# Chunk products of a state-space layer laid on two halves of TensorE's columns

## The chip, the cores and the metric

The kernel runs on one core of one Trainium2 chip. The metric is device time in microseconds of one execution. A profiled execution gives, beside its own time, a trace of every engine: TensorE (PE for its matmuls, PEld for its weight loads), VectorE (DVE), ScalarE (ACT), GpSimd (POOL) and the queue that issues DMAs (SP). The span is the time from the first to the last instruction of that execution.

## The reference, cut to what matters

A sequence of 512 tokens with 1024 features goes through one Mamba-2 layer, a shared key/value projection, one layer of differential attention and a final norm, all in float32. The change lies in the Mamba-2 layer's scan. It has 8 groups of 4 heads, 64 values a head and a state of 128. Within a chunk, with `cb` the product of C and B and `decay` the causal decay between two tokens, the reference computes

```python
cb = jnp.einsum("blgn,bsgn->blsg", c_c, b_c)
y_diag = jnp.einsum("blsgr,bsgrp->blgrp", cb[..., None] * decay, x_c)
y_off = jnp.einsum("blgn,bgrpn->blgrp", c_c, state) * jnp.exp(acs)[..., None]
```

The reference scans chunks of 64 tokens. The kernel does the same sum over chunks of 128 tokens, 4 of them in the sequence. The change is in the product that gives `y_diag`, of a 128 x 128 matrix (source tokens by output tokens) with 128 x 64 values.

## The kernel before, in words

Everything runs on one core. Large projections (`pz`, `pg`, `po`, `pq`, `pk`, `pt`, `pv`, `pb`, `pc`) are computed as three products each of operands split into a high and a low part in the format fp32r (`mm3`, line 217). ScalarE writes the high part of a weight tile (`whi`), VectorE the low one (`wlo`). The smaller products of the scan are plain f32; the profile shows each of these as two weight loads and two matmuls, and each fp32r product as one of either.

The work of the scan is in `ssd(g)` (line 536), called once for each of the 8 groups (lines 629 to 631). In between, a generator (`stream_a`, line 505) supplies the projections in the order of `order_a` (line 90). The projections of the group that comes next and the output projections are independent of the running scan, so TensorE has them to work on while other engines prepare the scan's operands. Most of the order on each engine in this first part is set by the planner of the tile framework, which simulates the program when it is built and puts each engine's instructions into a fixed queue; a few stretches are kept in program order by hand (`Ordered`, lines 43 to 58).

In `ssd(g)`:

- `pcb` (lines 542 to 545) holds B and C multiplied, 128 x 128 for each of the 4 chunks.
- `decays` (line 516) has filled `dec` with the causal decays of 4 heads and 4 chunks; VectorE multiplies `pcb` into it (lines 565 and 566).
- `xdt` (line 559) holds the scaled values, with 128 source tokens on the partitions and 64 values a head.
- `bt`, `xe`, `psA`, `psB` and `hst` (lines 546 to 579) carry the state from chunk to chunk.
- Lines 584 to 591 form the products inside a chunk. A bank `pyd` of PSUM holds two chunks: for each of its 2 chunks and 4 heads, one product takes `dec[:, h, c, :]` as the stationary operand (128 source tokens by 128 output tokens) and moves `xdt[:, c, h, :]` (128 source tokens by 64 values). The result has 128 output tokens on the partitions and 64 columns. After 8 products VectorE adds the bank to `dx` (line 591).
- `po1` and `po2` (lines 595 to 599) give the part that comes from the state; the rest of the function gates, normalizes and transposes the result (`pyt`, line 622) into `yT` for the output projection.

Eight groups with two banks each make 16 banks `pyd` and 128 products. Nearly all instructions carry line 53 in the profile, the line of the recording helper, so the tiles' names tell them apart.

Of the kernel before, what the change touches and what calls it, by code (L numbers as in the profile page):

```python
# [24 lines left out]
HD = 64  # L25
# [36 lines left out]
def trunk(ctx, tc, x, x_t, par, w_dt, w_in, w_out, w_kvqg, w_bo, d_skip, lam_qk, fin_g, out):  # L62
    nc = tc.nc
    V, A, T = (Ordered(tc, e) for e in (nc.vector, nc.scalar, nc.tensor))
# [14 lines left out]
    def ss_bank(name):  # L79
        turns[0] += 1  # L80
        tag = "mm" if turns[0] % turns[1] >= 3 else "ss"
        return psum.tile([P, 512], F32, tag=tag, name=name, bufs=3 if tag == "ss" else 4)
# [453 lines left out]
    def ssd(g):  # L536
        bc, cc, x0, x1 = conv_out.pop(g)
        xc = (x0, x1)
        dec, een = decs.pop(g)
# [11 lines left out]
        xdt = bp.tile([P, NQ, R, HD], F32, tag="xdt", name=f"xdt{g}")  # L551
# [31 lines left out]
        pyd = []  # L583
        for q in range(2):
            pyd.append(ss_bank(f"pyd{g}_{q}"))
            for c in (2 * q, 2 * q + 1):
                for h in range(R):
                    o = (c % 2) * 256 + h * HD
                    T.matmul(pyd[q][:, o:o + HD], lhsT=dec[:, h, c, :], rhs=xdt[:, c, h, :], start=True, stop=True)
            dq = dx[:, 2 * q:2 * q + 2].rearrange("p c h e -> p c (h e)")  # L590
            V.tensor_tensor(out=dq, in0=pyd[q].rearrange("p (c e) -> p c e", c=2), in1=dq, op=ALU.add)
        if g % 2 and g < G - 1:
# [36 lines left out]
    for g in range(G):  # L629
        until(f"g{g}")  # L630
        ssd(g)
# [266 lines left out]
    def half(t, n):  # L898
        hs = slice(n * 512, (n + 1) * 512)
        return x_tok[:, t, hs], fg[:, hs], ot[t][:, hs], out[t * P:(t + 1) * P, hs]  # L900
# [45 lines left out]
    h = DH - 1  # L946
# [53 lines left out]
    y, f, o, dst = half(3, 0)  # L1000
# [69 lines left out]
```

## Time and profile before

| | before |
|---|---|
| median of 3 runs | 741.71 us (741.63 to 741.74) |
| the profiled execution's own time | 741.54 us |
| its span, first to last instruction | 739.4 us |
| TensorE matmuls busy, instructions | 725.5 us, 3741 |
| weight loads busy, instructions | 606.6 us, 3741 |
| VectorE busy | 531.6 us |
| ScalarE busy | 444.8 us |
| GpSimd busy | 114.7 us |
| mean granted TensorE clock | 0.998 |

Busy time counts the time in which at least one instruction of the engine is under way. Matmuls are pipelined: a matmul's duration reaches from its start to a modelled end, and the next one starts before that end. So a row's mean duration is longer than the distance between two starts, and the distance is what a row of matmuls costs. In the form of a TensorE row, "128\*128" is the part of the array that it uses (rows by columns) and "128x64" what it moves (partitions by columns). In a timeline row the first number is the start and the second the time until the end of the last of the instructions merged into it.

### The profile page before, as it was taken

Reading aid. Unit: us, or ns where it says so; the run is one execution under the profiler, and the core shown is the slowest. Engines: PE = TensorE matmul, PEld = TensorE weight load, DVE = VectorE, ACT = ScalarE, POOL = GpSimd, SP = SyncE. Lnnn points to the kernel's source line nnn. Section 1 sums busy time; section 2 is a strip of 40 time slices with the busy share of each in tenths; the row PEclk is TensorE's granted clock in tenths of the full one; section 3 lists DMA queues with packets and bytes.
Section 4 is the critical chain, followed back from the end, with each engine's and each line's share of the span. In section 5 each row is a group of like instructions: output and inputs, shape, how many; then the busy total and the mean of one; then the engine's idle time right before and its main releaser. Section 6 shows DMA issues by size and latency. Waiting matters only on the chain.

```text
span 739.4 us, 10330 instructions
## 1 busy us (share of the span) xinstructions
PE 725.5 (98%) x3741; PEld 606.6 (82%) x3741; DVE 531.6 (72%) x1197; ACT 444.8 (60%) x969; POOL 114.7 (16%) x158
## 2 busy tenths in 40 slices
PE   9999999999999999999999999999999999999995
PEld 7787878888887888887888879888898898888874
DVE  5479955799668669469896655666767857785876
ACT  6749763765819457256443357666766766755565
POOL 0108241402234141150110101000000000000002
PEclk9999999999999999999999999999999999999999
DMA  8533313134131323132213220331221131121002
GB/s 310 215 129 160 114 58 115 57 114 171 58 114 58 115 114 100 72 115 80 92 58 113 74 97 8 114 114 58 66 106 57 58 115 58 58 104 68 28 1 113
DMA packets 12914, 70.83 MB, mean 96 GB/s; under 512 B 1600, under 2 KB 2112, under 8 KB 5312
## 3 DMA queue, kind: packets, MB, share of 16 engines
q1 hardware_dynamic: 12576, 70.06, 26.2%
q8 instruction: 29, 0.48, 0.3%
q14 instruction: 21, 0.17, 0.1%
q10 hardware_dynamic: 288, 0.12, 0.1%
HBM read 68.02 MB, written 2.16 MB: 95 GB/s over the span
## 4 chain that ended last, share of the span: by engine, by line
PE 77%; DVE 8%; ACT 7%; issue 5%; DMA 2%; POOL 1%; SPq 0%; ACTq 0%; POOLq 0%
PE pg L53 15%; PE po L53 13%; PE pt L53 7%; PE pz L53 7%; PE pq L53 6%; PE pv L53 6%; PE pk L53 6%; PE pyd L53 4%; PE pb L53 3%; PE sc L53 3%; DVE wlo L53 2%; PE pc L53 2%; ACT whi L53 2%; ACT L53 2%; DVE xc L53 1%
## 5 line engine op out<-in xcount | busy, mean ns | idle before, releaser
L53 DVE SCALAR_TENSOR_TENSOR wlo<-raw,prm,whi 128x512 fp32r<-128x512 f32 (+1 forms) x256 | 150.2, 634 | 51.2 <-ACT whi L53 50.8
L53 ACT ACTIVATE whi<-raw,prm 128x512 fp32r<-128x512 f32 (+1 forms) x256 | 136.8, 605 | 58.4 <-PE pz L53 14.1
L53 PE MATMUL pg<-a_hi,whi 128*128 128x512 f32 x256 | 102.5, 402 | 0.5 <-DVE xc L53 0.4
L53 PE MATMUL pg<-a_hi,wlo 128*128 128x512 f32 x256 | 102.7, 405 | 0.0
L53 PE MATMUL pg<-a_lo,whi 128*128 128x512 f32 x256 | 101.4, 397 | 0.0
L53 DVE SCALAR_TENSOR_TENSOR xc<-pg,prm,xc 128x511 f32<-128x511 f32 (+2 forms) x96 | 69.9, 741 | 5.6 <-ACT xc L53 4.8
L53 PEld LDWEIGHTS pg<-a_hi,whi 128*128 128x128 f32 x256 | 48.2, 188 | 11.9 <-issue 0.8
L53 PEld LDWEIGHTS pg<-a_hi,wlo 128*128 128x128 f32 x256 | 48.1, 188 | 10.9
L53 PEld LDWEIGHTS pg<-a_lo,whi 128*128 128x128 f32 x256 | 48.2, 188 | 10.7
L53 PE MATMUL po<-whi,yh 128*128 128x512 f32 x128 | 51.0, 401 | 0.6 <-ACT yh L53 0.6
L53 PE MATMUL po<-wlo,yh 128*128 128x512 f32 x128 | 51.0, 401 | 0.4 <-DVE wlo L53 0.4
L53 PE MATMUL pz<-wlo,a_hi 128*128 128x512 f32 x128 | 50.9, 398 | 0.0
L53 PE MATMUL pz<-whi,a_lo 128*128 128x512 f32 x128 | 50.9, 399 | 0.0
L53 PE MATMUL pz<-whi,a_hi 128*128 128x512 f32 x128 | 49.8, 402 | 0.1
L53 PE MATMUL po<-whi,yl 128*128 128x512 f32 x128 | 50.0, 397 | 0.0
L53 ACT ACT_TABLE_LOAD x33 | 42.3, 1283 | 10.3 <-DVE xc L53 7.7
L916 POOL TENSOR_TENSOR ot<-ot,fg 128x512 f32<-128x512 f32 x4 | 5.5, 1400 | 257.9 <-ACT ot L53 257.9
L53 ACT ACTIVATE s<-s,mx 128x128 f32<-128x128 f32 (+3 forms) x64 | 35.5, 557 | 9.5 <-DVE mx L53 9.2
L564 POOL TENSOR_TENSOR xe<-xdt,tok 128x256 f32<-128x256 f32 x24 | 15.4, 672 | 153.5 <-DVE xdt L53 153.5
L53 DVE CUSTOM_DVE_ANT_0 s<-sc,bias 128x128 f32<-128x128 f32 (+3 forms) x64 | 29.4, 488 | 12.3 <-PE sc L53 11.8
L53 PE MATMUL pv<-whi,b_hi 128*128 128x256 f32 x128 | 36.6, 286 | 0.0
L53 ACT ACTIVATE tmp<-dx 128x256 f32<-128x256 f32 x32 | 13.1, 410 | 38.7 <-DVE dx L53 38.7
(240 smaller groups left out, 1754.1 us busy)
## 6 DMA issues: line engine op xcount, KB each, us to landing
raw<-in_w_in SPq DMA_DIRECT2D x23, 1024.0 KB, 4.9
raw<-in_w_kvqg SPq DMA_DIRECT2D x16, 1024.0 KB, 4.8
dec<-acs_d SPq DMA_DIRECT2D x8, 1024.0 KB, 4.7
raw<-in_w_out SPq DMA_DIRECT2D x8, 1024.0 KB, 4.7
raw<-in_w_bo SPq DMA_DIRECT2D x4, 1024.0 KB, 4.8
xt<-in_x_t SPq DMA_DIRECT2D x8, 256.0 KB, 6.1
x_tok<-in_x SPq DMA_DIRECT2D x4, 512.0 KB, 8.7
out<-ot SPq DMA_DIRECT2D x8, 256.0 KB, 2.1
```

The costliest lines, as they stand in the source:

```text
L53: i = op(*args, **kw)
L564: GP.tensor_tensor(out=xe[:, c], in0=xdt[:, c], in1=toe_tok[:, c, hs].unsqueeze(2).to_broadcast([P, R, HD]), op=ALU.mult)
L916: GP.tensor_tensor(out=o, in0=o, in1=f, op=ALU.mult)
```

## The change

Each product of a chunk and a head is issued as two. The first takes the first 64 columns of `dec[:, h, c, :]` as the stationary operand and writes to partitions 0 to 63 of the bank, the second takes the other 64 and writes to partitions 64 to 127. Both move the same `xdt[:, c, h, :]` over all 128 source tokens. Each of them so occupies 64 columns of the array, the first or the second half. The two halves of one product are issued one after the other. Nothing else is edited.

```diff
             for c in (2 * q, 2 * q + 1):
                 for h in range(R):
                     o = (c % 2) * 256 + h * HD
-                    T.matmul(pyd[q][:, o:o + HD], lhsT=dec[:, h, c, :], rhs=xdt[:, c, h, :], start=True, stop=True)
+
+                    for r in (slice(0, 64), slice(64, 128)):
+                        T.matmul(pyd[q][r, o:o + HD], lhsT=dec[:, h, c, r], rhs=xdt[:, c, h, :], start=True, stop=True)
             dq = dx[:, 2 * q:2 * q + 2].rearrange("p c h e -> p c (h e)")
```

## The prediction

> **What bounds the kernel now.** I read the head of the profile page first, then the answer for the tile `pyd`, then the chain that ended last, then the timeline of TensorE around one block of the changed products. The head:
>
> ```profile
> span 739.4 us, 10330 instructions
> PE 725.5 (98%) x3741; PEld 606.6 (82%) x3741; DVE 531.6 (72%) x1197; ACT 444.8 (60%) x969; POOL 114.7 (16%) x158
> PEclk9999999999999999999999999999999999999999
> PE 77%; DVE 8%; ACT 7%; issue 5%; DMA 2%; POOL 1%; SPq 0%; ACTq 0%; POOLq 0%
> ```
>
> TensorE is busy for 98% of the span, its clock is granted in full throughout, and 77% of the chain lies on it. VectorE, the next engine, has 28% of its time free. So the kernel is bound by TensorE, and what TensorE wins or loses should appear in the total almost one for one, as long as the other engines can follow. For the stretch in which the changed products lie, first and last stage and the sum:
>
> ```profile
> core 0: us, PE busy (x) PEld busy (x) DVE busy (x) ACT busy (x) POOL busy (x), PEclk, DMA share, GB/s
> 50.00:100.00 50.00, 49.58 (x246) 40.74 (x245) 44.78 (x68) 32.17 (x49) 25.93 (x33) 1.00 0.39 147
> ...
> 350.00:420.00 70.00, 70.00 (x356) 58.71 (x355) 53.02 (x95) 27.16 (x52) 8.62 (x13) 1.00 0.25 90
> sum 370.00, PE 367.99 PEld 303.91 DVE 279.26 ACT 206.91 POOL 101.19; mean PE 52.57 PEld 43.42 DVE 39.89 ACT 29.56 POOL 14.46
> ```
>
> Of 370 us TensorE idles 2.0. VectorE works 279.3, so a stage shorter by as much as 12 us would still leave it at 78%. It is not the next bound. The answer for `pyd`:
>
> ```profile
> L53 PEld LDWEIGHTS pyd<-xdt,dec x256: 187/192/192, 79.6 to 419.1; 128*128 128x128 f32 x128
> L53 PE MATMUL pyd<-xdt,dec x256: 217/275/275, 79.8 to 419.1; 128*128 128x64 f32 x128
> L53 DVE TENSOR_TENSOR dx<-pyd,dx x16: 678/682/692, 82.3 to 419.4; 128x512 f32<-128x512 f32 x16
> ...
> who waited for it (us, times):
>   DVE dx L53: 7.2, 5
> ```
>
> Durations are minimum, median and maximum in ns. There are 8 groups times 4 chunks times 4 heads = 128 products, and 256 loads and 256 matmuls: each f32 product is two loads of 128 columns and two matmuls that move 64 columns. They come in 16 blocks of 8 products, one for each bank `pyd`, each followed by one addition on VectorE. The chain shows a block as one piece; first and last:
>
> ```profile
> 79.94 1.73 PE pyd L53 x16
> ...
> 417.67 1.75 PE pyd L53 x16
> ```
>
> A block is 1.74 us, so a load with its matmul takes 1.74 / 16 = 0.109 us, a product 0.218, and all sixteen blocks 27.8 us. That is all that the change can touch: 3.8% of the span.
>
> **Which half of the pair is the limit.** The products C^T B (`pcb`) have the same two full loads, but move 128 columns and not 64; the transposes into `pyt` use a load of the same columns in one pass:
>
> ```profile
> L53 PE MATMUL pcb<-xc,xc x64: 271/275/275, 65.6 to 373.8; 128*128 128x128 f32 x64
> L53 PEld LDWEIGHTS pyt<-ident,tmp x64: 137/140/144, 108.2 to 433.3; 128*128 128x128 f32 x64
> L53 PE MATMUL pyt<-ident,tmp x64: 270/273/330, 108.2 to 433.4; 128*128 128x128 f32 x64
> ```
>
> A `pyd` matmul that waits for nothing takes 217 ns, one of `pcb` 271: 64 columns more cost 54 ns, so I put the moving part of a `pyd` matmul at 54 ns. But its median is 275, 58 ns more than its minimum: it waits for its weights. The weight load is the limit, at 0.109 us for 128 f32 columns, and the matmul array streams for half of that time. The transposes' loads are 192 - 140 = 52 ns shorter. A load of half the work should therefore take 109 - 52 = 57 ns. The timeline after a stall gives it directly:
>
> ```profile
> 108.16 0.20 PEld L53 LDWEIGHTS pyt<-ident,tmp 128*128 128x128 f32 x2 [0.51 <-ACT tmp L53]
> 108.16 0.33 PE L53 MATMUL pyt<-ident,tmp 128*128 128x128 f32 x1
> ```
>
> Two loads in 0.20 us, of which the second is 0.14 long: it starts 0.06 after the first. So 57 to 60 ns for a short load. I use it for a load of 64 f32 columns, which has half of the columns of a full one; no row shows that form itself.
>
> **The change part by part.** Removed: 256 loads of 128 columns and their 256 matmuls. Added: 512 loads of 64 columns and 512 matmuls that still move 64 columns, since every half reads the whole `xdt` slice. The loaded columns are the same in number, the moved columns double. Nothing is moved past another queue: SP, POOL, ACT and VectorE get the same instructions, and VectorE's addition still waits for the last matmul of a block. Per block it is 32 pairs instead of 16. The price hangs on whether the two column halves of the array work side by side.
>
> First the pairs. Within one half of the array a load can be no shorter than 57 to 60 ns and a matmul 54, so each half of the array needs 16 x 0.06 = 0.96 us for its 16 pairs. If the halves overlap, the order low half twice, high half twice lets the last pair of one product's half run beside the first of the next, which gives 17 slots: 1.02 us instead of 1.74. That saves 0.72 in a block and 11.5 us in all. If they don't overlap, the 32 loads follow each other: 32 x 0.057 = 1.82 to 32 x 0.06 = 1.92, which costs 0.08 to 0.18 a block, 1.3 to 2.9 us in all.
>
> Then the changeover. Every matmul of the kernel before is on 128 columns of the array ("128*128"), and a block of half-width ones now stands between full-width ones, sixteen times. In the kernel before a load always runs behind the matmul ahead of it:
>
> ```profile
> 79.34 0.59 PE L53 MATMUL psB<-xe,bt 128*128 128x256 f32 x2
> 79.56 1.97 PEld L53 LDWEIGHTS pyd<-xdt,dec 128*128 128x128 f32 x16
> 79.78 1.89 PE L53 MATMUL pyd<-xdt,dec 128*128 128x64 f32 x16
> 81.45 0.19 PEld L53 LDWEIGHTS pg<-a_hi,whi 128*128 128x128 f32 x1
> 81.48 0.48 PE L53 MATMUL pg<-a_hi,whi 128*128 128x512 f32 x1
> ```
>
> Each block's first load starts while the last `psB` matmul still runs. If the array has to be empty before its layout changes, this cover is gone twice a block. The tail of a matmul after its moving part is 217 - 54 = 163 ns; with the bare load behind it, entering costs 0.163 + 0.06 = 0.22 and leaving 0.163 + 0.109 = 0.27, in all 0.49 a block and 7.8 us for sixteen. The lower bound is nothing. Below nothing is excluded, since the loads are already hidden now. [...] I take the full price, since the stalls in this trace show a load exposed whenever nothing runs ahead of it.
>
> The sum against the profiled execution, which took 741.5 us (2.1 of it outside the span, 0.2 under the median of 741.7): 741.5 - 11.5 + 7.8 = 737.8 us. With a free changeover it would be 730.0. The addition on VectorE and what it feeds come a little earlier; five of the sixteen additions waited for `pyd` before, 7.2 us together, which is VectorE's idle time and not TensorE's. 128 more matrix products also pass the planner that orders the queues at build time, so a block may be cut in two; each cut would be another changeover of 0.49 us.
>
> **The rivals.** *The halves overlap* is my forecast: TensorE has the most to win there, and the matmul array is idle half the time in these blocks. Against it: each product's two passes are on the same half one after the other, so an in-order queue may hold the other half's load back.
>
> *The loads go one after another.* If the queue lets one load run at a time, as everywhere in this trace, nothing overlaps and the loads stay the limit: +1.3 to +2.9, and with the changeover +9.1 to +10.7. That is 742.8 to 752.2 us. This is the rival on the slower side: its place is the load port, its price is 0.06 us a pair and the changeover; it decides as soon as the starts of consecutive loads in a block are nowhere nearer than 0.05 us.
>
> *No load ahead of a matmul in flight.* If in half-width work a load waits until the running matmul has streamed, a pair is 0.06 + 0.054 = 0.114, a block 32 x 0.114 = 3.65, and the kernel 16 x 1.91 = 30.6 us longer: 772 us. The rows above speak against it for full-width work, where the load at 79.56 runs under the matmul at 79.34. [...]
>
> *A half load is no cheaper.* If 64 columns cost 0.109 like 128 and the two halves run side by side, a product is again two slots and the edit brings nothing: 741.5, or up to 749.3 with the changeover. The loads of 128 columns with two different durations (140 and 192) speak for a cost by work, so this is unlikely.
>
> **How the numbers follow.** A measurement of this kernel can tell about 0.2%, 1.5 us, from no change. Overlap gets 0.46, all of it faster: 730.0 to 737.8. Loads in a row gets 0.36: 0.08 of that is its lowest price with no changeover, within 0.2%, and 0.28 is slower. No load ahead gets 0.12, slower. The half load at full price gets 0.06: 0.04 the same, 0.02 slower. Together faster 0.46, same 0.12, slower 0.42. Signs are mixed; the likeliest case's own range is 729.5 to 738. The range for 8 in 10 runs from 729.5 to the top of the loads in a row, 752; left out are the 0.12 at 772 and a few hundredths beyond either end.
>
> **What would show it.** The profile after should list 512 loads and 512 matmuls for `pyd`, in a form with 64 columns of the array. Under my forecast a block of 32 pairs takes about 1.0 us between its first and last matmul, loads of the two halves start within some 30 ns of each other, and the first load of a block comes 0.2 us after the matmul ahead has streamed. Loads in a row show as a steady 0.057 to 0.06 us between loads. I am wrong if blocks are longer than 1.74 us, if the full-width matmuls around them lengthen, or if TensorE's idle time grows by more than the blocks shrink.

## The result, and the profile after

The kernel with the change takes 748.28 us (median of 4 runs, 747.76 to 749.88) against 741.67 us (4 runs, 741.18 to 741.74): a ratio of 1.0096 [1.0084, 1.0108]. It is slower, by 6.6 us between the medians and by 6.2 to 8.0 in the interval of the ratio. The forecast was 3.9 us faster. The profiled execution of the kernel after took 747.76 us, its span is 746.0. The head of its page, the lines that answer to those of before:

```profile
span 746.0 us, 10830 instructions
PE 722.3 (97%) x3997; PEld 596.3 (80%) x3997; DVE 535.3 (72%) x1197; ACT 439.5 (59%) x965; POOL 115.7 (16%) x158
PEclk9999999999998999999999999999999999999999
PE 79%; DVE 10%; issue 5%; ACT 4%; DMA 2%; POOL 1%; SPq 0%; ACTq 0%; POOLq 0%
```

Four things are to be seen. TensorE has 256 matmuls and 256 loads more, as it should. It is busy 3.2 us less than before (725.5), so the edit did save work. The span is 6.6 us longer all the same, so TensorE idles about 10 us more: 746.0 - 722.3 = 23.7 against 739.4 - 725.5 = 13.9. And the thirteenth digit of the clock row is an 8: around 235 us the granted clock was not full.

The blocks themselves did what was forecast. First the two rows of the tile `pyd`, then TensorE's timeline around the block whose rows of before the prediction shows, loads after matmuls, and last its first two loads alone:

```profile
L53 PEld LDWEIGHTS pyd<-xdt,dec x512: 132/138/138, 79.4 to 424.1; 128*64 128x64 f32 x171
L53 PE MATMUL pyd<-xdt,dec x512: 222/222/271, 79.4 to 424.2; 128*64 128x64 f32 x171
```

```profile
78.85 0.59 PE L53 MATMUL psB<-xe,bt 128*128 128x256 f32 x2
79.37 1.15 PE L53 MATMUL pyd<-xdt,dec 128*64 128x64 f32 x32
80.45 0.50 PE L53 MATMUL pg<-a_hi,whi 128*128 128x512 f32 x1
...
79.37 1.01 PEld L53 LDWEIGHTS pyd<-xdt,dec 128*64 128x64 f32 x32 [0.33 <-PE psA L53]
80.45 0.19 PEld L53 LDWEIGHTS pg<-a_hi,whi 128*128 128x128 f32 x1
...
79.37 0.14 PEld L53 LDWEIGHTS pyd<-xdt,dec 128*64 128x64 f32 x2 [0.33 <-PE psA L53]
```

Thirty-two loads end 1.01 us after the first starts, the last being 0.138 long: one starts every (1.01 - 0.138) / 31 = 0.028 us. Loads run two at a time (the first two lie within 0.14 us, each 0.13 to 0.138 long), and the median matmul is as short as the shortest, 222 ns: it no longer waits for its weights. From the end of the last `psB` matmul to the end of the first `pg` matmul it was 81.96 - 79.93 = 2.03 us and is now 80.95 - 79.44 = 1.51. So a block gains 0.52 us with its changeovers in it, and sixteen should gain 8.3.

What took this back lies elsewhere, and the granted clock shows where to look. Busy time of each engine in three consecutive stretches of the kernel after, cut where the clock changes:

```profile
core 0: us, PE busy (x) PEld busy (x) DVE busy (x) ACT busy (x) POOL busy (x), PEclk, DMA share, GB/s
225.00:237.40 12.40, 7.82 (x38) 6.15 (x36) 12.40 (x17) 8.82 (x14) 7.45 (x8) 1.00 0.22 85
237.40:244.20 6.80, 4.67 (x11) 3.70 (x12) 5.57 (x15) 3.38 (x6) 0.00 (x0) 0.50 0.43 154
244.20:250.00 5.80, 5.80 (x31) 4.81 (x31) 3.07 (x5) 3.10 (x6) 0.00 (x0) 1.00 0.00 0
```

The same 25 us in the kernel before had no such stretch, and TensorE ran 115 matmuls in them, where it now runs 38 + 11 + 31 = 80:

```profile
225.00:250.00 25.00, 23.97 (x115) 18.99 (x114) 21.89 (x42) 22.53 (x35) 4.40 (x7) 1.00 0.24 85
```

TensorE's timeline there in the kernel after; the square bracket gives the idle time ahead of a row and what ended it:

```profile
232.43 0.40 PE L53 MATMUL po<-whi,yl 128*128 128x512 f32 x1
239.53 0.79 PE L53 MATMUL po<-whi,yh 128*128 128x512 f32 x1 [6.71 <-DVE x_tok L53]
240.13 0.63 PE L53 MATMUL po<-wlo,yh 128*128 128x512 f32 x1
240.55 0.63 PE L53 MATMUL po<-whi,yl 128*128 128x512 f32 x1
...
244.32 0.40 PE L53 MATMUL po<-whi,yl 128*128 128x512 f32 x1
244.56 0.39 PE L53 MATMUL po<-whi,yh 128*128 128x512 f32 x1
```

TensorE stands still for 6.71 us, and behind the wait its matmuls start 0.43 us apart until 244, where 0.24 follows. The bank that the next tile of this output projection (`po`) needs comes free when VectorE has added an earlier tile to `x_tok`: the row puts the wait down to that addition. VectorE's timeline in that time:

```profile
232.38 2.46 DVE L53 TENSOR_TENSOR dec<-dec,pcb 128x512 f32<-128x512 f32 x4
234.77 1.40 DVE L53 SCALAR_TENSOR_TENSOR wlo<-raw,prm,whi 128x512 fp32r<-128x512 f32 x2
...
236.82 1.40 DVE L53 SCALAR_TENSOR_TENSOR wlo<-raw,prm,whi 128x512 fp32r<-128x512 f32 x2
...
238.81 1.27 DVE L53 TENSOR_TENSOR x_tok<-po,x_tok 128x512 f32<-128x512 f32 x2
```

VectorE isn't idle: the table above has it busy for all of the 12.40 us. Its two additions simply stand late in its queue, behind four products into `dec`, four low parts `wlo` and two steps of `xc`. In the kernel before, VectorE makes the same two additions 2 us later still, and yet TensorE doesn't wait for them. The first `po` row of this projection before, then the additions, and last the first `po` row after:

```profile
230.72 0.72 PE L53 MATMUL po<-whi,yh 128*128 128x512 f32 x2
240.96 1.28 DVE L53 TENSOR_TENSOR x_tok<-po,x_tok 128x512 f32<-128x512 f32 x2
...
226.97 0.72 PE L53 MATMUL po<-whi,yh 128*128 128x512 f32 x2
```

So the additions are not late. TensorE came to this projection 3.75 us earlier, and it stopped after two tiles of it, 24 matmuls, where before it ran three, 36 matmuls, and then transposes ahead of the fourth. The traces show how far the order was changed. With `pyd` set aside, I looked for the longest run of rows, by tile and form, that stands in the same order in both kernels: it leaves out 187 of TensorE's 3,485 matmuls, 123 of VectorE's 1,197 instructions and 78 of ScalarE's 969. My count from start to start of TensorE's rows, by tile, gives `pyd` 27.5 us before and 17.3 after, but `po` 118.3 and 128.5, `pz` 91.6 and 95.9, `pg` 184.9 and 186.8, `psA` with `psB` 8.1 and 9.4.

My theory: the split gains about 8 us, and the planner, given another program, lays all queues in another order that costs about twice that. The rivals: the split itself costs time around its blocks through its changeovers, or the new order is harmless and the wait at 232 us comes from TensorE being ahead of the others.

### The profile page after: what moved, and what is told of

Its sections match the earlier page's. It is cut to its first block, busy times and chain, and to the rows that moved or that the text cites. A ratio compares the mean times of both kernels' runs of the same rounds, so it can differ in the third digit from the quotient of the medians.

```text
span 746.0 us, 10830 instructions
## 1 busy us (share of the span) xinstructions
PE 722.3 (97%) x3997; PEld 596.3 (80%) x3997; DVE 535.3 (72%) x1197; ACT 439.5 (59%) x965; POOL 115.7 (16%) x158
## 4 chain that ended last, share of the span: by engine, by line
PE 79%; DVE 10%; issue 5%; ACT 4%; DMA 2%; POOL 1%; SPq 0%; ACTq 0%; POOLq 0%
PE pg L53 16%; PE po L53 14%; PE pz L53 9%; PE pt L53 7%; PE pq L53 6%; PE pv L53 6%; PE pk L53 6%; DVE wlo L53 3%; PE pb L53 3%; PE sc L53 3%; PE pyd L53 2%; PE pc L53 2%; DVE xc L53 1%; ACT whi L53 1%; PE psA L53 1%
## 5 line engine op out<-in xcount | busy, mean ns | idle before, releaser
L53 DVE SCALAR_TENSOR_TENSOR wlo<-raw,prm,whi 128x512 fp32r<-128x512 f32 (+1 forms) x256 | 155.1, 653 | 37.4 <-ACT whi L53 36.8
L53 PE MATMUL po<-whi,yh 128*128 128x512 f32 x128 | 52.8, 415 | 7.3 <-DVE x_tok L53 6.7
L53 PEld LDWEIGHTS pg<-a_hi,whi 128*128 128x128 f32 x256 | 48.2, 188 | 12.3 <-ACT xc L53 0.7
L53 PE MATMUL pz<-whi,a_hi 128*128 128x512 f32 x128 | 51.7, 417 | 1.2 <-ACT whi L53 1.2
L53 ACT ACT_TABLE_LOAD x29 | 37.2, 1283 | 17.3 <-DVE xc L53 7.9
L53 DVE CUSTOM_DVE_ANT_0 s<-sc,bias 128x128 f32<-128x128 f32 (+3 forms) x64 | 29.3, 488 | 12.3 <-PE sc L53 11.8
L53 ACT ACTIVATE xc<-pg,prm 128x512 f32<-128x512 f32 x32 | 24.5, 770 | 22.4 <-DVE pg L53 22.4
L53 DVE TENSOR_TENSOR x_tok<-po,x_tok 128x512 f32<-128x512 f32 x32 | 21.6, 684 | 21.3 <-PE po L53 21.3
```

The costliest lines, as they stand in the source:

```text
L53: i = op(*args, **kw)
```

## The experiments

In the first group the order was separated from the split. The plan was made from one version of the products, and the instructions of the other were then held to that plan's order in all five queues, with the second half of a product directly behind the first. The diffs in this section are cuts of the kernels' own lines, and "..." stands for what is left out.

**The split in the order of before.** The program is built unsplit first, and its order is given to the split one as order edges that carry no semaphore:

```diff
+    for changed in (False, True):
...
+            names = trunk(tc, *args, o, changed=changed, order=order)
...
+                    tc.add_manual_dep(i, last.name, mybir.DependencyInfo(mybir.DependencyClass.NoSync, ...), ...)
```

> The changed products, each half directly behind the other, with every engine's queue held in the order of the kernel before. Theory A (the halves do overlap; a block with its two changeovers takes 0.50 us less of TensorE than before, 1.28 instead of 1.78; the loss of the changed kernel is the new order that the planner chose): 741.7 - 16 x 0.50 = 733.7 us, no wait of TensorE over 1.1 us, the clock granted in full until the end. Theory B (the loss comes from the split itself: earlier blocks leave TensorE waiting for VectorE and ScalarE whatever the order): near the changed kernel's 748 us, with the wait for x_tok still there.

It took 734.29 us (733.95 to 735.23) against 741.11 for the kernel before beside it: 0.9905 [0.9888, 0.9921], a gain of 5.9 to 8.3 us. Its page, and two rows of its waits (total, times and longest, in us):

```profile
span 733.1 us, 10842 instructions
PE 718.1 (98%) x3997; PEld 592.8 (81%) x3997; DVE 532.6 (73%) x1197; ACT 444.6 (61%) x969; POOL 115.3 (16%) x158
PEclk9999999999999999999999999999999999999998
```

```profile
PE po L53 <- DVE wlo L53: 1.0, 1, 1.0
PEld po L53 <- DVE x_tok L53: 0.5, 1, 0.5
```

The wait for `x_tok` is 0.5 us, no digit of the clock row drops before the end, and TensorE is busy 718.1 us, 7.4 less than before. Its trace has every row of TensorE, VectorE and ScalarE outside `pyd` in the order of before. This version beats both kernels. The split is a gain, which rules out the rival that its changeovers cost more than it saves.

**The order of after without the split.** The reverse: the plan is made from the split program, the products run whole.

```diff
-    for changed in (False, True):
+    for changed in (True, False):
```

> The products unsplit, as before, but every engine's queue in the order that the planner chose for the changed kernel. Theory A (order alone costs): 748.3 + 8.0 = 756.3 us, with a wait for x_tok of several us near 240 us and a halved clock behind it. Theory B (the order costs nothing, the split does): 741.7 us.

754.70 us (753.95 to 755.31): 1.0181 [1.0166, 1.0196], 13.4 us slower at the ratio. TensorE's row for the wait is that of the kernel after:

```profile
PE po L53 <- DVE x_tok L53: 6.7, 1, 6.7
```

So the wait comes with the order and needs no split. The two parts add up: -7.0 + 13.4 = +6.4 us, where the whole change gave +7.1 at its ratio. What holding the queues costs in itself was not run alone; that the two parts come within 0.7 us of the whole leaves little room for it.

**Halves apart.** In the order of before, each bank gets its 8 low halves first and then its 8 high halves; against the first kernel of this section:

```diff
+                for r in (slice(0, 64), slice(64, 128)):
+                    for c in (2 * q, 2 * q + 1):
+                        for h in range(R):
...
-                    for r in (slice(0, 64), slice(64, 128)):
```

> Order of before; in each bank first the low halves of all 8 products, then the high halves of all 8. Theory A1 (the queue starts work in order, so only neighbours in the queue overlap): 16 pairs follow each other on one half, then 16 on the other, 32 x 0.057 + 0.15 = 1.97 us a block instead of 1.08, 14 us over the first run: about 748 us. Theory A2 (the array takes work for the idle half from further back in the queue): as the first run, 734 us.

744.55 us (744.13 to 744.95): 1.0045 [1.0030, 1.0059], 10.3 us over that first kernel. A block in the timeline, its first 13 loads, all its loads and its matmuls:

```profile
79.19 0.83 PEld L53 LDWEIGHTS pyd<-xdt,dec 128*64 128x64 f32 x13 [0.33 <-PE psA L53]
...
79.19 1.76 PEld L53 LDWEIGHTS pyd<-xdt,dec 128*64 128x64 f32 x32 [0.33 <-PE psA L53]
79.19 1.90 PE L53 MATMUL pyd<-xdt,dec 128*64 128x64 f32 x32
```

The same 32 pairs take 1.76 us where they took 1.01. Thirteen loads of one half in a row start (0.83 - 0.138) / 12 = 0.058 us apart, which is the price that the prediction had taken from the transposes (0.057 to 0.06). The whole block has (1.76 - 0.138) / 0.058 = 28 such steps, not 31: by my estimate from this the first three loads of the high half run beside the last three of the low one. So in this block the queue reached about three pairs ahead, a little further than the neighbours of Theory A1 (1.97 us a block, about 748 us), and far less than Theory A2 needs. Without the alternation of the halves in the queue the split loses time; its gain comes from the alternation.

**Alternating layouts.** Heads 0 and 2 at full width, heads 1 and 3 split, in the order of before: the layout changes eight times in a block and not twice.

```diff
-                    if not changed:
+                    if not changed or h % 2 == 0:
                         T.matmul(pyd[q][:, o:o + HD], lhsT=dec[:, h, c, :], rhs=xdt[:, c, h, :], start=True, stop=True)
```

> Order of before; in each bank full-width products (heads 0 and 2) and split ones (heads 1 and 3) alternate, so there are four changeovers in and four out per bank instead of one. Theory A (each entry costs 0.15 us and each exit 0.20): a block takes 4 x 0.218 + 4 x 0.115 + 4 x 0.35 = 2.73 us instead of 1.74, 16 us more than before: about 758 us. Theory B (a changeover costs next to nothing): 4 x 0.218 + 4 x 0.115 = 1.33 us, 735 us.

752.06 us (751.44 to 752.41): 1.0145 [1.0130, 1.0160], between the two theories and nearer to A. The row of a block's loads, and that of the load behind it:

```profile
79.24 2.56 PEld L53 LDWEIGHTS pyd<-xdt,dec 128*128 128x128 f32 x24
81.87 0.19 PEld L53 LDWEIGHTS pg<-a_hi,whi 128*128 128x128 f32 x1
```

The trace merges the two forms into one row here. From first load to the load behind the block it is 81.87 - 79.24 = 2.63 us; in the unsplit kernel it is 81.45 - 79.56 = 1.89. Four products at half the slots should have saved 4 x 2 x (0.109 - 0.058) = 0.41, so the four changes in and out cost 2.63 - 1.89 + 0.41 = 1.15, or 0.29 us for one in and out. The other way to it, from the kernel after: 16 slots of (1.01 - 0.138) / 15 = 0.058 are 0.93 us, their gain over 1.74 is 0.81, and 0.52 of it is left: again 0.29.

The second group asks what in the new order costs the time.

**Only TensorE's queue held, only VectorE's queue held.** The split, with one of the five queues in the order of before and the others as the planner then lays them.

```diff
-PINNED = 'PE DVE Activation Pool SP'
+PINNED = 'PE'
```

> Split as in the changed kernel, TensorE's queue held in the order of before, the planner free on all other engines. If the loss lies in the order of TensorE's queue (output projections put where their banks wait for VectorE's additions): near the first run, 734 to 737 us. If it lies in the order of the other queues: near 748 us.

739.44 us (10 runs, 738.78 to 740.47): 0.9979 [0.9970, 0.9989]. TensorE held alone brings back most of the loss, but not all: a new wait appears, 3.7 us of it in one piece, and the mean granted clock of the profiled execution is 0.995, where the first kernel of this section has 0.997:

```profile
PE pg L53 <- DVE xc L53: 4.1, 2, 3.7
```

```diff
-PINNED = 'PE'
+PINNED = 'DVE'
```

> Split as in the changed kernel, VectorE's queue held in the order of before, the planner free on all other engines. If the loss lies in the order of VectorE's queue (the additions into x_tok behind weight splits): 734 to 737 us. If it lies in TensorE's own order: near 748 us.

759.11 us (758.68 to 759.60): 1.0245 [1.0230, 1.0260], worse than the change itself. TensorE's waits are now spread over many places:

```profile
PE pyt L53 <- ACT tmp L53: 5.3, 2, 3.4
...
PE pg L53 <- ACT zs L53: 3.6, 2, 2.9
PE pz L53 <- DVE xc L53: 3.3, 1, 3.3
PE po L53 <- DVE wlo L53: 3.1, 1, 3.1
```

The planner laid TensorE's queue anew here, neither as before nor as in the change (by the count used above, 174 and 179 of its matmuls stand out of line), so this is a third order and not the change's with VectorE's put back. Neither kernel came out where its expectation had it. The loss doesn't sit in VectorE's queue alone, and TensorE's explains most of it but not all.

**Split in half of the groups, no order held.** Two kernels split only groups 0 to 3, or only groups 4 to 7; the second has `g >= 4` in this line:

```diff
-for r in (slice(0, 64), slice(64, 128)):
+for r in (slice(0, 64), slice(64, 128)) if g < 4 else (slice(0, 128),):
```

> Only groups 0 to 3 split, no order held, the planner free everywhere. By the price of a block, 6.8 us over 16 blocks, the eight split blocks win 3.4 us. Theory A (the planner's new order costs in single places, above all the wait for x_tok near 235 us, which lies behind these groups): 741.1 - 3.4 + about 10 = 748 us. Theory B (the loss is shared by all split blocks alike): half of the changed kernel's loss, 744.5 us.

746.40 us (746.09 to 746.52): 1.0073 [1.0058, 1.0088].

> Only groups 4 to 7 split, no order held. The first half of the order is as before, so the wait near 235 us shouldn't be there. Theory A: 741.1 - 3.4 + 0 to 3 = 738 to 741 us. Theory B (the loss is shared by all split blocks alike): 744.5 us.

737.85 us (737.14 to 738.42): 0.9957 [0.9943, 0.9972]. Half of the same edit costs 5.4 us, the other half gains 3.2. The first lies between its two theories, and the second just below its Theory A, far from B. TensorE's order differs from before in 137 matmuls in the first and 31 in the second, by the count used above, and only the first shows the known wait:

```profile
PE po L53 <- DVE x_tok L53: 6.4, 1, 6.4
```

**Two additions moved.** The change with its own order, but for VectorE's queue, where the two additions to `x_tok` that TensorE waits for stand ahead of the first and of the third of the four products into `dec`:

```diff
+            for what, where in ((("x", 0, 0, 0), ("dec", 4, 0)), (("x", 0, 0, 1), ("dec", 4, 2))):
+                seq.remove(place[MARK[what]])
+                seq.insert(seq.index(place[MARK[where]]), place[MARK[what]])
```

> The changed kernel in the order that its own planner chose, with two of VectorE's additions into x_tok (the first two of the first output projection) moved a few places ahead in VectorE's queue, in front of the products of dec and pcb. Theory A (the single wait for x_tok and the halved clock behind it are most of the order's price): the wait of 6.7 us shrinks to about 0.5 and the 11 or so matmuls at 0.43 instead of 0.23 us go, 748.3 - 6.2 - 2.1 = 740 us. Theory B (VectorE is simply late by then, and TensorE will wait elsewhere for it): 745 to 748 us.

742.26 us (10 runs, 740.16 to 743.72): 1.0013 [1.0003, 1.0023], some 6 us under the change. VectorE's and TensorE's timelines:

```profile
232.50 0.69 DVE L53 TENSOR_TENSOR x_tok<-po,x_tok 128x512 f32<-128x512 f32 x1
...
234.30 0.68 DVE L53 TENSOR_TENSOR x_tok<-po,x_tok 128x512 f32<-128x512 f32 x1
```

```profile
238.71 0.40 PE L53 MATMUL po<-whi,yl 128*128 128x512 f32 x1
241.01 0.47 PE L53 MATMUL po<-whi,yh 128*128 128x512 f32 x1 [1.90 <-DVE y_c L53]
```

TensorE now runs through to 239. The wait of 1.90 us there is put down to another instruction of VectorE (`y_c`): TensorE does wait elsewhere for it, as Theory B had it, but far shorter; the clock still drops behind it (0.63, 0.50, 0.50 and 0.66 in the four us from 242), which at half the clock is 3.4 us and not 6.8. The time lies between the two theories, nearer to A. Two instructions in another place of VectorE's queue are worth 6 us. It also answers the rival on TensorE being ahead: the engine is no slower and the wait is gone, so the place in the queue makes the wait.

**Quarters.** In the order of before, each product as four, on 32 columns each:

```diff
-for r in (slice(0, 64), slice(64, 128)):
+for r in [slice(n, n + 32) for n in range(0, 128, 32)]:
```

> Order of before; each product laid as four, on 32 columns of the array each. Theory A (with halves side by side the moved columns are now the limit, 0.054 to 0.058 us a matmul on each part of the array, and four parts work side by side): a block stays at 1.08 us, 734 us. Theory B (the start of each pair costs TensorE's queue about 0.02 us or more in turn): 64 pairs x 0.02 = 1.3 us a block, 738 us or more. Theory C (four loads at once don't run): 1.9 us a block, 748 us.

736.50 us (735.63 to 738.70): 0.9939 [0.9919, 0.9958]. Its interval overlaps that of the halves, so neither is shown to be better. A block:

```profile
79.82 0.94 PEld L53 LDWEIGHTS pyd<-xdt,dec 128*32 128x32 f32 x64 [0.33 <-PE psA L53]
79.83 1.10 PE L53 MATMUL pyd<-xdt,dec 128*32 128x64 f32 x64
```

64 loads take 0.94 us, hardly less than 32 at half width. A load is 0.110 long. If four start within 0.02 us, an estimate from the 0.006 between the loads of two halves in the kernel after, each quarter's 16 pairs stand (0.94 - 0.11 - 0.02) / 15 = 0.054 us apart. That is what the prediction gave the moved columns (54 ns). I read it so that they are the limit once the loads run side by side, and that further cuts have nothing left to win; no run varies the moved columns alone.

## Why the prediction was wrong, point by point

**The slots of a block: right.** The forecast was 17 slots of 0.06, 1.02 us, where 1.08 was measured in the chain. That two halves work side by side, on which the 11.5 us of the sum rest, no row of the kernel before shows; the kernel after shows the first two loads starting within 0.01 us, and 16 slots of 0.058, not 17. The queue so seems to take the high half's first load past the low half's second pass; the records don't name the halves. By these slots the pairs save (1.74 - 0.93) x 16 = 13.0 us. The condition set for the first rival, loads nowhere nearer than 0.05 us, isn't met, which rules out loads in a row; the block of 1.08 us rules out the third rival and its 772 us; a half load of 0.058 us rules out the one at full price. The 748.28 us do lie in the stretch that the first rival was given (742.8 to 752.2), but by coincidence: nothing of its mechanism is there. That one load runs at a time "as everywhere in this trace" holds for the kernel before only of starts: they lie 0.11 us apart in a block and 0.06 in the transposes, where a load is 0.19 and 0.14 long.

**The changeover: right in kind, too dear.** 0.49 us a block was the forecast, taken at its upper end; 0.29 was measured in two ways. By my estimate from the starts of single instructions, entering takes about 0.10 us in which nothing starts (the last `psB` matmul starts at 79.06, its like are 0.215 apart, and the first load comes at 79.37) and 0.05 of a bare load, leaving about 0.10 and 0.105; together that is 0.35, somewhat over the net price of 0.29. The tail of 0.163 us that the prediction charged for each way isn't paid whole. Over sixteen blocks this is 3.2 us in the change's favour. No run shows that the array has to be empty before its layout changes, on which the 7.8 us of the sum rest; what the runs showed in their place is 0.29 us a block, 4.6 us for sixteen.

**The gain of the edit alone: right in sign, under by half.** The edit by itself was forecast at -11.5 + 7.8 = -3.7 us. In the order of before it measured -7.0 (-5.9 to -8.3); from the timeline it is 16 x 0.52 = 8.3 us.

**The failed step: the order of the queues.** The prediction wrote "Nothing is moved past another queue: SP, POOL, ACT and VectorE get the same instructions", and of the planner only that with 128 more products "a block may be cut in two". The first is true of the list of instructions and false of their order. No block is cut: the chain of the kernel after has them whole, for example

```profile
211.28 1.08 PE pyd L53 x32
...
217.92 1.08 PE pyd L53 x32
```

But elsewhere the planner changed the order of hundreds of instructions on three engines, and that term, set at zero, measures +13.4 us (12.3 to 14.5 from the interval). The sum with what the runs showed is 741.5 - 7.0 + 13.4 = 747.9 us, against 747.76 for the profiled execution, closer than the intervals of about 1 us on each term can promise. Of the conditions under which the prediction called itself wrong, the one on TensorE's idle time is near: it grew by 9.8 us, more than the 8.3 that the blocks gained with their changeovers, though not more than the 10.2 by which the rows of `pyd` alone shrank. The case behind this condition had no price and no chance.

The 13.4 us can be followed into the trace. The split in the order of before has the same instructions, and the kernel after has a span 746.0 - 733.1 = 12.9 us longer. TensorE idles 23.7 - 15.0 = 8.7 us more, 6.7 of them in one wait, and is busy 722.3 - 718.1 = 4.2 us more. For the 4.2 the clock is the cause in sight: at half of it (0.50) from 237.40 to 244.23 some eleven `po` matmuls started 0.43 us apart and not 0.233, about 2.1 us, and two shorter stretches at half the clock, of 3.41 us each, begin at 295.43 and 438.79 us. Ahead of the first fall TensorE stood still, from 232.82 on. Ahead of the other two it didn't: in the 3.41 us before them, a time as long as the stretches themselves, it worked for 1.48 and 1.67 us:

```profile
292.02:295.43 3.41, 1.48 (x8) 0.64 (x6) 2.33 (x4) 3.40 (x7) 0.00 (x0) 1.00 0.00 0
435.38:438.79 3.41, 1.67 (x10) 0.78 (x8) 1.14 (x7) 1.71 (x4) 0.00 (x0) 1.00 0.84 281
```

So 4.58 us of standing still went ahead of the first fall, and 1.93 us (two waits) and 1.74 us (one) of 3.41 ahead of the others; what makes the clock fall isn't shown. The split in the order of before, whose single waits stay at or under 1.0 us behind the first one of 1.5, has a clock of 1.00 from 50 to 420 us, and only the last digit of its row is lower. The long wait so cost more than its length here: 6.71 us and 2.1.

**What stays open.** Why the planner prefers the new order was not looked into: which of its prices makes TensorE take the output projection early is unknown, so the runs show that the order costs the time, not what would have to be changed in the planner. Nor was it tried to join the two blocks of a group, which would save one changeover in two.

## What to carry to other kernels

Where a build-time planner lays the queues, an edit of one engine's instructions can change the order on all of them: price it with the order held, and count the reshuffle as a term of its own, which here was twice the edit's gain (+13.4 against -7.0 us). Where TensorE was the bound (98% of the span) and the moved part short against its weight load (54 against 109 ns by the prediction's estimate), laying products on halves of the columns paid: a ratio of 0.9905 with the halves alternating in the queue, but 1.0045 with one half's in a row and 1.0145 with half of the products split and four changeovers of 0.29 us in a block. After such an edit read the granted clock first: here the one digit below full led straight to the longest wait. The two falls of 3.4 us show in no digit of that row, only in the mean (0.989 against 0.998).

## What the runs showed of the hardware that was not expected

Loads of f32 weights on two halves of the columns started within 0.01 us of each other where they alternated in the queue (0.028 us a load on average), and 0.058 us apart where one half's loads stood in a row, by my estimate with three pairs of each half side by side where one half's row ends and the other's begins. On quarters it was (0.94 - 0.11) / 63 = 0.013 us a load. In the kernel after the granted clock fell to half (0.50) behind 3.41 us in which TensorE had worked for 1.48 us. A change of layout and back cost 0.29 us, less than the tails of the matmuls and the bare loads together (0.49 by the prediction's estimate).
